# Key block of the retention branch moved behind a product of another item, gate stores on ScalarE's queue, value stores issued one group later

## The chip, the cores and the metric

The kernel runs on one core of a Trainium2 chip. The metric is the device time of one execution in microseconds (us); the median of several timed runs counts. The engines are named as the profile names them: PE (TensorE, matmuls), DVE (VectorE), ACT (ScalarE), POOL (GpSimd) and SP (SyncE, which only issues transfers here).

## The reference, cut to what matters

Two layers of a trunk over a sequence of 512 rows of 1024 float32 channels. Each layer begins with one wide projection of x, and the work around the change is this projection:

```python
for l in range(DEPTH):                                  # DEPTH = 2
    h = jnp.einsum('bsd,de->bse', x, w_in[l])
    rq, rk, rv, rg, cq, ck, cv, dq, dk, dv, gates = jnp.split(h, splits, axis=-1)
    o_a = _retention(rq, rk, rv, rg, ret_norm_g[l])     # rotary on rq and rk, 4 heads
    o_b = _chunk_attention(cq, ck, cv, ca_rel_bias[l])
    o_c = _diff_attention(dq, dk, dv, lam, lambda_init, da_norm_g[l])
    g = jax.nn.sigmoid(gates + b_merge[l]).reshape(B, S, N_BRANCHES, D)
    merged = sum(g[:, :, i] * (o_i @ w_i) for each of the three branches)
    x = _layer_norm(DEEPNORM_ALPHA * x + merged @ w_out[l], ...)
    x = _layer_norm(DEEPNORM_ALPHA * x + swiglu_ffn(x), ...)
```

## The kernel before, in words

**Numbers and weights.** Every float32 operand is carried as a pair of float32r tiles, a high half and a low half (names ending in h and l), and a float32 product is three matmuls (`mm3`, lines 122 to 124). Weights are streamed. A block of 1 MB (128 partitions by 2048 numbers) is loaded by a DMA from SP's queue into one of 4 staging tiles `st`, ACT copies its high half to `wh` and DVE subtracts to get the low half `wl` (line 271 and 272; 154 and 155 for blocks of 256 columns). The split pairs come from a pool of 3 (`AHEAD`), so a block can be split only when the third last has been used up by PE.

**Products from sums.** Four weight quarters and four quarters of x make one 2 by 2 product in seven block products rather than eight (Strassen-Winograd): `m1`, `m2`, `y`, `v`, `x`, `g`, `h`. The items of a projection pair carry a letter and one of these names: `w` projects the values CV and DV, `e` the gate of branch 0, `p` and `q` the retention's RV and RG. `m1`, `m2` and `h` use plain x on PE; `y` and `x` need the left sums of x (`s12`, function `s_left`), `v` and `g` the right sums (`s43`, `s_right`), which DVE and ACT make. Weight sums are made either by DVE in the staging tile (lines 233, 239 and 260) or by an accumulating DMA on POOL's queue (`more`, line 178). A letter with `a` or `c` (`w.a`, `w.c`, `e.c`, `p.a`) is such a load made ahead: `e.c`, for example, loads the block of `e.g` and accumulates a second quarter into it. PSUM results are copied by ACT (`tc`, line 761), combined by DVE (lines 766, 771 and 776) and passed on: values are split once more and stored to DRAM (`v_away`, line 882), gate halves go through a tanh and are stored (`gate_part`, line 1080; `gate_done`, line 1069, for other gates).

**Retention's queries and keys.** RQ and RK are blocks of 256 columns each. Their PSUM results go through a rotary (`rotary`, lines 400 to 404: ACT copies, DVE multiplies and adds) and a split (`rqkh`, `rqkl`). In both layers the item `u_first` makes both blocks of the first two heads. In layer 0 it is also the start of the program: `first_blocks` issues the loads of both weight blocks in quarters of 256 KB, with one tile of the transposed input xT between each two, and the splits of these in the same alternation (lines 613 and 614 for xT).

**What sets the order.** The kernel holds a list of items (`start` and the list behind it, from line 1143); `run_items` walks it in program order, fetches the weights of coming items ahead, and after each half of an item `between` runs a group of side work (sums, loads ahead, the second layer's layer-norm outputs in natural order, `natural`). A scheduler then reorders instructions within each engine's stream by its own priorities, keeping dependencies; every engine and every DMA queue runs its stream in order.

Of the kernel before, what the change touches and what calls it, by code (L numbers as in the profile page):

```python
# [17 lines left out]
P = 128  # L18
# [38 lines left out]
def trunk(ctx, tc, x_in, xT_in, w_in, ret_norm_g, da_norm_g, lq1, lk1, lq2, lk2, w_a, w_b, w_c, b_merge, w_out,  # L57
# [506 lines left out]
    pending = []  # L564

    def between():

        if pending:
            for fn in pending.pop(0):
                fn()  # L570
# [28 lines left out]
    def first_blocks(*specs):  # L599

        wts = [Wt(*sp, later=True) for sp in specs]
        for k in range(0, KT, 2):
            for i, wt in enumerate(wts):
                wt.load(k, k + 2)
                xfs[0][k + i] = g(name="xf")
                nc.sync.dma_start(xfs[0][k + i], xT_in[P * (k + i):P * (k + i) + P])
        for k in range(0, KT, 2):
            for i, wt in enumerate(wts):
                src, pr = xfs[0][k + i], Pair("xT")
                xTs[0][k + i] = pr  # L610
                for ins in wt.split(k, k + 2):
                    tc.keep_in_program_order(ins)
                tc.keep_in_program_order(nc.scalar.copy(pr.hi, src))
                tc.keep_in_program_order(nc.vector.tensor_sub(pr.lo, src, f(pr.hi)))  # L614
        return wts
# [9 lines left out]
    def layer(l):  # L625
# [82 lines left out]
        def u_first():  # L708

            def fn(*wts):  # L710
                banks = [[bank("pt") for _ in range(2)] for _ in range(2)]
                if l == 0:
                    ret_tables()
                    for k in range(KT):
                        for w, b in zip(wts, banks):
                            for j in range(2):
                                a, c = xT[k], slice(P * j, P * j + P)
                                mm3(b[j], w.hi[:, k, c], w.lo[:, k, c], a.hi, a.lo, k == 0, k == KT - 1)
                    quarters(0)
                    for k in range(4):  # L720
                        s_left(k)()
                    vectors()
                for i, w in enumerate(wts):
                    for j in range(2):
                        if l:
                            proj_T(xT, w, P * j, ps=banks[i][j])
                        rqk_done((rq, rk)[i], j, banks[i][j])
                        between()

            return [([wcols(c, 256)], KT) for c in (RQ, RK)], fn  # L730
# [140 lines left out]
        def v_away(dst, wd):  # L871


            def done(t, c):
                for hf in range(2):
# [6 lines left out]
                    nc.sync.dma_start(dst[t, hf], f(s))  # L882
# [180 lines left out]
        def gate_done(br, d, ps, away=True):  # L1063
# [3 lines left out]
            if away:  # L1067
                th[br, d] = dram.tile([P, 512], F32, name=f"th{l}_{br}_{d}")
                nc.sync.dma_start(th[br, d], t)

        def gate_part(br, d, hf, c):
# [3 lines left out]
            for i in range(2):  # L1075
# [4 lines left out]
                nc.sync.dma_start(th[br, d + i][:, 256 * hf:256 * hf + 256], s[:, o])  # L1080
# [62 lines left out]
        if l == 0:  # L1143
            start = [(u_first(), [], [], [w["a"]], [columns]), (w["m1"], [s_right(0)], [s_right(1)]),
                     (w["m2"], [s_right(2)], [s_right(3)]), (e["m1"],), (e["m2"], [w["c"]]), (w["y"], [lam]), (w["v"],)]
        else:
            turned, natural = ([functools.partial(fn, i) for i in range(4)] for fn in hooks[l])
            start = [(w["m1"], [ret_tables, vectors], turned[:2]), (w["m2"], turned[2:]),
                     (u_first(), [w["a"], s_left(0)], [s_left(1), s_left(2)], [s_left(3)], [columns]),
                     (e["m1"], [s_right(0)], [s_right(1)]), (e["m2"], [s_right(2), w["c"]], [s_right(3)]),  # L1150
                     (w["y"], [natural[0]], [natural[1]]), (w["v"], [natural[2], lam], [natural[3]])]
# [323 lines left out]
```

## Time and profile before

| | |
|---|---|
| timed runs, median (lowest to highest) | 1929.14 us (1928.84 to 1929.17), 3 runs |
| the profiled execution's own time | 1930.13 us |
| its span in the profile | 1928.0 us, granted clock 0.987 |
| PE busy | 1871.7 us, 97% |
| DVE, ACT, POOL busy | 1374.2, 991.9, 130.5 us |
| DMA | 306.07 MB, 159 GB/s in the mean |

How to read the rows of the profile that follow: a row of a timeline is start, duration, engine, line, operation, output and inputs, number of instructions, and in brackets the engine's idle time just before it with the instruction that ended that idle time. A row of windows gives for a stretch its length, then each engine's busy time and number of instructions, the granted TensorE clock as a share of full speed, the DMA engines' share and GB/s. A row of the groups gives busy time and mean nanoseconds of one instruction, then the idle time before them. Tile names are those of the program without their numbers: `pf` and `pt` are PSUM banks of block products and of projections, `psr` of the retention's scores.

### The profile page before, as it was taken

How to read it: one execution, taken by the hardware profiler on the slowest of the kernel's cores; microseconds unless marked ns; L12 is line 12 of the kernel's file. 1: busy time of each engine (PE TensorE's matmuls, PEld its weight loads, DVE VectorE, ACT ScalarE, POOL GpSimd, SP SyncE). 2: the span in 40 equal slices, each digit the busy share in tenths (PEclk: the TensorE clock that was granted, in tenths of full speed). 3: DMA queues.
4: the chain of work that ended last, by engine and by line, in shares of the span. 5: the costliest groups of instructions: out<-in, count | busy, mean ns of one | idle time of the engine just before them, and what ended most of it. 6: DMA issues, size and time to landing. Idle time of an engine off the chain costs nothing. (4 is left out here: it accounts for less than half of the span.)

```text
span 1928.0 us, 24006 instructions
## 1 busy us (share of the span) xinstructions
PE 1871.7 (97%) x9090; PEld 1573.8 (82%) x9090; DVE 1374.2 (71%) x2069; ACT 991.9 (51%) x1605; POOL 130.5 (7%) x153
## 2 busy tenths in 40 slices
PE   9879999999999999999997799999999999999998
PEld 7768888888888888888886688888888888888886
DVE  6747766767766777888688577666677667778886
ACT  5545555566743544654264454555676435455541
POOL 2000000000000000010020000000000000100100
PEclk9989999999999999999998899999999999999999
DMA  9787344332235676787377863443421456777871
GB/s 285 190 248 199 98 150 151 93 132 77 66 131 153 174 187 187 180 230 204 127 189 212 240 187 108 138 137 110 136 77 45 153 157 171 181 190 204 210 196 44
DMA packets 223283, 306.07 MB, mean 159 GB/s; under 512 B 8900, under 2 KB 111392, under 8 KB 223168
## 3 DMA queue, kind: packets, MB, share of 16 engines
q1 hardware_dynamic: 192832, 245.40, 38.3%
q0 software_dynamic: 30336, 59.15, 17.8%
q8 instruction: 71, 1.16, 0.2%
q14 instruction: 44, 0.36, 0.1%
HBM read 281.39 MB, written 23.12 MB: 158 GB/s over the span
## 5 line engine op out<-in xcount | busy, mean ns | idle before, releaser
L272 DVE TENSOR_TENSOR wl<-st,wh 128x2048 fp32r<-128x2048 f32 x140 | 320.2, 2290 | 147.6 <-ACT wh L271 147.0
L271 ACT CAST wh<-st 128x2048 fp32r<-128x2048 f32 x140 | 267.2, 1911 | 240.1 <-PE pf L124 101.9
L122 PE MATMUL pt<-xTh,wh 128*128 128x512 f32 x832 | 327.0, 394 | 1.1 <-ACT wh L154 0.9
L123 PE MATMUL pt<-xTl,wh 128*128 128x512 f32 x832 | 324.1, 389 | 1.9 <-DVE xTl L614 1.9
L124 PE MATMUL pt<-xTh,wl 128*128 128x512 f32 x832 | 324.3, 390 | 0.0
L155 DVE TENSOR_TENSOR wl<-st,wh 128x1024 fp32r<-128x1024 f32 (+1 forms) x188 | 200.1, 1084 | 60.6 <-ACT wh L154 54.6
L154 ACT CAST wh<-st 128x1024 fp32r<-128x1024 f32 (+1 forms) x188 | 172.3, 940 | 111.7 <-PE pt L123 34.3
L123 PEld LDWEIGHTS pt<-xTl,wh 128*128 128x128 f32 x832 | 156.4, 188 | 33.4 <-DVE xTl L614 2.2
L124 PEld LDWEIGHTS pt<-xTh,wl 128*128 128x128 f32 x832 | 156.2, 188 | 33.0
L122 PEld LDWEIGHTS pt<-xTh,wh 128*128 128x128 f32 x832 | 156.2, 188 | 33.0 <-ACT wh L154 1.4
L122 PE MATMUL pf<-wh,xTh 128*128 128x512 f32 x336 | 132.8, 395 | 1.5 <-ACT rph L106 0.8
L123 PE MATMUL pf<-wl,xTh 128*128 128x512 f32 x336 | 131.3, 391 | 0.5 <-DVE wl L272 0.3
L124 PE MATMUL pf<-wh,xTl 128*128 128x512 f32 x336 | 131.0, 390 | 0.0
L761 ACT COPY tc<-pf 128x512 f32<-128x512 f32 x96 | 54.9, 588 | 76.1 <-PE pf L124 69.7
L123 PE MATMUL pf<-wl,s12h 128*128 128x512 f32 x224 | 87.7, 391 | 3.2 <-DVE wl L272 3.2
L122 PE MATMUL pf<-wh,s12h 128*128 128x512 f32 x224 | 87.9, 395 | 1.6 <-ACT wh L271 1.6
L122 PE MATMUL pf<-wh,s43h 128*128 128x512 f32 x224 | 87.4, 390 | 0.0
L124 PE MATMUL pf<-wh,s12l 128*128 128x512 f32 x224 | 87.3, 390 | 0.0
L123 PE MATMUL pf<-wl,s43h 128*128 128x512 f32 x224 | 87.2, 389 | 0.0
L124 PE MATMUL pf<-wh,s43l 128*128 128x512 f32 x224 | 87.2, 389 | 0.0
L122 PEld LDWEIGHTS pf<-wh,xTh 128*128 128x128 f32 x336 | 63.1, 188 | 16.5 <-ACT rph L106 1.6
L123 PEld LDWEIGHTS pf<-wl,xTh 128*128 128x128 f32 x336 | 63.2, 188 | 13.5 <-DVE wl L272 1.5
(338 smaller groups left out, 4082.7 us busy)
## 6 DMA issues: line engine op xcount, KB each, us to landing
st<-in_w_in SPq DMA_DIRECT2D x62, 1024.0 KB, 5.2
st<-in_w_ffn_in SPq DMA_DIRECT2D x38, 1024.0 KB, 5.7
st<-in_w_in POOLq DMA_DIRECT2D x20, 1024.0 KB, 10.4
st<-in_w_ffn_in POOLq DMA_DIRECT2D x20, 1024.0 KB, 10.8
st<-in_w_ffn_out SPq DMA_DIRECT2D x20, 1024.0 KB, 7.5
st<-in_w_in SPq DMA_DIRECT2D x32, 512.0 KB, 5.0
st<-in_w_ffn_out POOLq DMA_DIRECT2D x16, 1024.0 KB, 9.0
st<-in_w_ffn_in SPq DMA_DIRECT2D x24, 512.0 KB, 6.4
```

The lines of the kernel that those rows point to most:

```text
L122: nc.tensor.matmul(ps, lh, rh, start=start, stop=False, skip_group_check=onto)
L123: nc.tensor.matmul(ps, lh, rl, start=False, stop=False, skip_group_check=onto)
L124: nc.tensor.matmul(ps, ll, rh, start=False, stop=stop, skip_group_check=onto)
L154: return [nc.scalar.copy(self.hi[:, a:b], self.st[:, a:b]), nc.vector.tensor_sub(self.lo[:, a:b], self.st[:, a:b], f(self.hi[:, a:b]))]
L155: nc.vector.tensor_sub(self.lo[:, a:b], self.st[:, a:b], f(self.hi[:, a:b]))]
L271: nc.scalar.copy(self.hi, st)
L272: nc.vector.tensor_sub(self.lo, st, f(self.hi))
L761: nc.scalar.copy(t[to, j], ps)
```

## The change

It has four parts. (1) `u_first` makes only the RQ block and is used only in layer 0; `first_blocks` therefore starts the program with one weight block and all eight xT tiles. (2) RK becomes an item of its own (`u_rqk(rk, RK, 0)`) and comes behind `w.y`, so that `w.m1`, `w.m2`, `e.m1` and `e.m2`, which need no sums of x, stand ahead of `w.y`. The items behind it change places: before `w.v, w.x, e.y, w.g, e.v, w.h, p.m1`, now RK, `w.v, e.y, w.x, e.v, w.g, p.m1, w.h`. In layer 1 RQ is an item of its own too, and the side work (`columns`, the sums, `natural`) is handed to later groups. (3) The value stores of `v_away` are put in a list and issued by `between` one group later, still on SP's queue. (4) The gate stores `th` are issued from ACT's queue (`nc.scalar.dma_start`) instead of SP's.

```diff
 def between():
+    for fn in stores.pop(0):
+        fn()
+    stores.append([])
     if pending:
...
-    def first_blocks(*specs):
-        wts = [Wt(*sp, later=True) for sp in specs]
+    def first_blocks(spec):
+        wt = Wt(*spec, later=True)
         for k in range(0, KT, 2):
-            for i, wt in enumerate(wts):
-                wt.load(k, k + 2)
-                xfs[0][k + i] = g(name="xf")
+            wt.load(k, k + 2)
+            for i in (k, k + 1):
+                xfs[0][i] = g(name="xf")
...
-            return [([wcols(c, 256)], KT) for c in (RQ, RK)], fn
+            return [([wcols(RQ, 256)], KT)], fn
...
-                    nc.sync.dma_start(dst[t, hf], f(s))
+                    stores[-1].append(functools.partial(nc.sync.dma_start, dst[t, hf], f(s)))
...
-                nc.sync.dma_start(th[br, d], t)
+                nc.scalar.dma_start(th[br, d], t)
...
-                nc.sync.dma_start(th[br, d + i][:, 256 * hf:256 * hf + 256], s[:, o])
+                nc.scalar.dma_start(th[br, d + i][:, 256 * hf:256 * hf + 256], s[:, o])
...
         if l == 0:
-            start = [(u_first(), [], [], [w["a"]], [columns]), (w["m1"], [s_right(0)], [s_right(1)]),
-                     (w["m2"], [s_right(2)], [s_right(3)]), (e["m1"],), (e["m2"], [w["c"]]), (w["y"], [lam]), (w["v"],)]
+            start = [(u_first(), [], [w["a"]]), (w["m1"], [], [s_right(0)]), (w["m2"], [columns], [s_right(1)]),
+                     (e["m1"], [], [s_right(2)]), (e["m2"], [s_right(3)], [w["c"]]), (w["y"], [lam])]
...
-                     (w["y"], [natural[0]], [natural[1]]), (w["v"], [natural[2], lam], [natural[3]])]
+                     (w["y"], [lam], [natural[0]])]
...
-            (w["x"],), (e["y"],), (w["g"], [p["a"]]), (e["v"], [e["c"]]), (w["h"],),
-            (p["m1"], [s_dh(0)]), (e["x"],), (p["y"], [], [s_r1(0)]), (e["g"],), (p["v"], [s_dh(1)], [p["c"]]), (e["h"],),
+            (u_rqk(rk, RK, 0), *([[natural[1]], [natural[2]]] if l else [])), (w["v"], *([[natural[3]]] if l else [])),
+            (e["y"],), (w["x"],), (e["v"], [p["a"]]), (w["g"], [e["c"]]), (p["m1"], [s_dh(0)]), (w["h"],), (e["x"],),
+            (p["y"], [], [s_r1(0)]), (e["g"],), (p["v"], [s_dh(1)], [p["c"]]), (e["h"],),
```

At the start of layer 0 the copy of the last xT tile's high half stands on ACT directly behind the split of w.m1's whole block, after the change as before.

**ACT in layer 0 around w.y.** Here is ACT's stream of before, from the third rotary of `u_first` (`sw`, `rqkh`) to the copies of e.m1 (`tc11_412` and `tc11_434` are w.m1's; `wh_571` is a split of the block in `st_569`):

```order
L400 COPY sw_355<-pt_189 64x512 x2
L271 CAST wh_571<-st_569 128x2048
L106 CAST rqkh_362<-rot_358 128x512
L400 COPY sw_369<-pt_190 64x512 x2
L106 CAST rqkh_376<-rot_372 128x512
L761 COPY tc11_412<-pf_399 128x512
L106 CAST s43h_417<-sb_414 128x512
L761 COPY tc11_434<-pf_421 128x512
L271 CAST wh_645<-st_569 128x2048
```

This is ACT's stream after the change, at the place where RK's work begins. `tc11_319` and `tc11_334` are w.m1's copies, `wh_561` is w.v's split, `wh_610` is e.y's, and `tc11_437` and `tc11_466` are the copies of e.m1:

```order
L760 COPY tc11_334<-pf_321 128x512
L106 CAST s43h_339<-sb_336 128x512
L271 CAST wh_561<-st_559 128x2048
L106 CAST vhl_363<-tc11_319 128x4x64
L106 CAST vhl_367<-tc11_319 128x4x64
L106 CAST vhl_391<-tc11_334 128x4x64
L106 CAST vhl_395<-tc11_334 128x4x64
L271 CAST wh_610<-st_299 128x2048
L106 CAST s43h_404<-sb_401 128x512
L760 COPY tc11_437<-pf_412 128x512
L760 COPY tc11_466<-pf_441 128x512
```

The third and fourth rotary are gone from this place, and the copies of e.m1 stand behind e.y's split. DVE's adds of e.m2 to these copies are what frees the PSUM banks that RK's matmuls use.

**POOL's accumulating transfers in layer 0.** These are six in a row of before: `st_392` in the first, third and fifth row is the block of chain e (the fifth makes e.h's), `st_609` is w.c's, `st_866` p.a's, and `st_924` in the last row is e.c's:

```order
L178 DMA st_392<-in_w_in 128x4x512
L178 DMA st_609<-in_w_in 128x4x512
L178 DMA st_392<-in_w_in 128x4x512
L178 DMA st_866<-in_w_in 128x4x512
L178 DMA st_392<-in_w_in 128x4x512
L178 DMA st_924<-in_w_in 128x4x512
```

The same stretch after the change, where `st_299` is the block of chain e, `st_556` w.c's, `st_864` p.a's and `st_918` e.c's:

```order
L178 DMA st_299<-in_w_in 128x4x512
L178 DMA st_556<-in_w_in 128x4x512
L178 DMA st_299<-in_w_in 128x4x512
L178 DMA st_864<-in_w_in 128x4x512
L178 DMA st_918<-in_w_in 128x4x512
L178 DMA st_299<-in_w_in 128x4x512
```

The last two have changed places: e.c's transfer no longer stands behind the one that makes e.h's block. In layer 1 the order of these two is as before.

**DVE in layer 1.** Here is DVE's stream of before around the add that frees a bank for e.y (`tc11_8525`, from e.m2); `z` are the passes of `natural`:

```order
L553 TENSOR_TENSOR z_7011<-z_7011,bc_7786 128x512
L404 TENSOR_TENSOR rot_8476<-rot_8476,sw_8473 128x512
L554 TENSOR_TENSOR z_7011<-z_7011,bc_7790 128x512
L553 TENSOR_TENSOR z_7012<-z_7012,bc_7787 128x512
L112 TENSOR_TENSOR rqkl_8481<-rot_8476,rqkh_8480 128x512
L304 TENSOR_TENSOR sb_8527<-xf_8090,sa_8351 128x256
L305 TENSOR_TENSOR sb_8527<-xf_8066 128x256
L766 TENSOR_TENSOR tc11_8525<-tc11_8525,pf_8575 128x512
L554 TENSOR_TENSOR z_7012<-z_7012,bc_7791 128x512
L553 TENSOR_TENSOR z_7013<-z_7013,bc_7786 128x512
```

And this is where the passes of `natural` begin after the change; `wl_8715` is the low half of w.x's split, `s43l_8569` the last of the right sums:

```order
L305 TENSOR_TENSOR sb_8565<-xf_8077 128x256
L686 TENSOR_TENSOR nlam_8601<-le_8599 128x1
L272 TENSOR_TENSOR wl_8715<-st_8572,wh_8714 128x2048
L112 TENSOR_TENSOR s43l_8569<-sb_8565,s43h_8568 128x512
L687 TENSOR_SCALAR nlam_8601<-nlam_8601 128x1
L553 TENSOR_TENSOR z_7004<-z_7004,bc_7779 128x512
L553 TENSOR_TENSOR z_7010<-z_7010,bc_7779 128x512
L554 TENSOR_TENSOR z_7004<-z_7004,bc_7783 128x512
L553 TENSOR_TENSOR z_7005<-z_7005,bc_7780 128x512
L402 TENSOR_TENSOR rot_8658<-pt_8630,cosr_8162 128x512
```

All passes of `natural` now come behind the adds of e.m2, the last sums and w.x's split, and RK's rotary stands among them.

More of the change, by code (lines that the diff above doesn't have):

```diff
@@ L564, in trunk @@
     pending = []
+    stores = [[], []]
     def between():
+        for fn in stores.pop(0):
+            fn()
+        stores.append([])
         if pending:
@@ L708, in u_first, with fn @@
         def u_first():
[L710 to L723, printed above, removed]
-                    for j in range(2):
[L725 to L728, printed above, removed]
-            return [([wcols(c, 256)], KT) for c in (RQ, RK)], fn
+            def fn(wt):
+                banks = [bank("pt") for _ in range(2)]
+                ret_tables()
+                for k in range(KT):
+                    for j in range(2):
+                        a, c = xT[k], slice(P * j, P * j + P)
+                        mm3(banks[j], wt.hi[:, k, c], wt.lo[:, k, c], a.hi, a.lo, k == 0, k == KT - 1)
+                quarters(0)
+                vectors()
+                for k in range(4):
+                    s_left(k)()
+                for j in range(2):
+                    rqk_done(rq, j, banks[j])
+                    between()
+            return [([wcols(RQ, 256)], KT)], fn
         def s_left(k):
```

18 lines of the change are left out of this document (9 added, 9 removed).

## The prediction

> **What bounds the kernel now.** I read the page first, then windows of the span, then the PE's waits, and last the timelines of the engines at the stretches that wait.
>
> ```profile
> span 1928.0 us, 24006 instructions
> PE 1871.7 (97%) x9090; PEld 1573.8 (82%) x9090; DVE 1374.2 (71%) x2069; ACT 991.9 (51%) x1605; POOL 130.5 (7%) x153
> ...
> core 0: us, PE busy (x) PEld busy (x) DVE busy (x) ACT busy (x) POOL busy (x), PEclk, DMA share, GB/s
> 0.00:240.00 240.00, 215.49 (x1115) 184.50 (x1116) 162.39 (x193) 124.13 (x177) 23.70 (x35) 0.96 0.73 204
> 240.00:960.00 720.00, 719.24 (x3430) 601.88 (x3429) 515.95 (x823) 372.92 (x623) 40.44 (x46) 1.00 0.53 150
> 960.00:1240.00 280.00, 258.48 (x1337) 220.63 (x1337) 199.88 (x258) 149.10 (x231) 24.68 (x29) 0.96 0.64 177
> 1240.00:1930.00 690.00, 678.50 (x3213) 566.76 (x3211) 495.96 (x796) 345.75 (x577) 41.65 (x45) 0.99 0.51 144
> ```
>
> The PE is the bound: it is busy for 1871.7 of 1928.0 us. The change leaves its matmuls as they are and can only alter the idle 56 us. The windows show where those lie: 24.5 us in the first 240 us (the start of layer 0) and 21.5 us between 960 and 1240 (the start of layer 1). The change works in exactly these two stretches. The granted clock is 0.96 there, so idle time costs twice: it is lost, and afterwards the PE runs slower.
>
> Smaller windows give each stall's price, as idle time plus busy time times the missing clock:
>
> ```profile
> 49.00:62.00 13.00, 8.50 (x49) 8.30 (x50) 12.16 (x18) 5.02 (x8) 1.27 (x1) 0.76 0.76 186
> 68.00:88.00 20.00, 17.00 (x97) 14.47 (x96) 12.73 (x16) 11.44 (x19) 1.27 (x1) 1.00 0.85 237
> 123.00:145.00 22.00, 10.84 (x59) 9.86 (x58) 13.61 (x13) 10.61 (x14) 1.28 (x1) 0.69 0.63 189
> 1010.00:1047.00 37.00, 26.96 (x126) 22.29 (x125) 32.29 (x48) 15.66 (x24) 1.27 (x1) 0.86 0.59 177
> 1081.00:1103.00 22.00, 11.66 (x60) 10.70 (x59) 13.39 (x13) 10.61 (x14) 1.28 (x1) 0.69 0.67 199
> ...
> 25.21 0.50 PE L123 MATMUL pt<-xTl,wh 128*128 128x512 f32 x1 [1.92 <-DVE xTl L614]
> 49.70 0.39 PE L122 MATMUL pf<-xTh,wh 128*128 128x256 f32 x1 [1.60 <-DVE rot L402]
> 49.93 0.28 PE L123 MATMUL pf<-xTl,wh 128*128 128x256 f32 x1
> 56.63 0.58 PE L122 MATMUL pf<-xTh,wh 128*128 128x256 f32 x1 [3.79 <-DVE rot L402]
> 57.01 0.41 PE L123 MATMUL pf<-xTl,wh 128*128 128x256 f32 x1
> ...
> 128.22 0.58 PE L122 MATMUL pf<-s43h,wh 128*128 128x256 f32 x1 [4.92 <-ACT wh L271]
> 136.27 0.48 PE L122 MATMUL psr<-rqkh 128*128 128x128 f32 x1 [4.71 <-DVE rtmp L817]
> 1029.23 0.55 PE L122 MATMUL pf<-s12h,wh 128*128 128x256 f32 x1 [3.53 <-DVE tc L766]
> 1033.21 0.58 PE L124 MATMUL pf<-s12h,wl 128*128 128x256 f32 x1 [3.22 <-DVE wl L272]
> ```
>
> Layer 0: e.m2 loses 13.0 − 8.5 = 4.5 us idle, 2.0 us at clock 0.76, and the 1.6 us before: 8.1. The stretch of w.x, e.y and w.v (68 to 88) loses 3.0. e.g (123 to 145) loses 11.2 idle and 0.31 × 10.84 = 3.4: 14.5. Layer 1: w.y to w.v (1010 to 1047) loses 10.0 + 3.8 = 13.8, e.g 10.3 + 3.6 = 13.9. These five places are 53 us. The gap of 3.79 us was followed by matmuls of 0.41 instead of 0.28 us; the one of 1.60 was not.
>
> **The change part by part.** *The start of layer 0.* One weight block less stands ahead of w.m1's block, but the last xT tile still waits behind it.
>
> ```profile
> 3.68 0.62 ACT L154 CAST wh<-st 128x512 fp32r<-128x512 f32 x1 [1.67 <-DMA st<-in_w_in]
> 20.32 1.91 ACT L271 CAST wh<-st 128x2048 fp32r<-128x2048 f32 x1 [4.08 <-DMA st<-in_w_in]
> 22.13 0.61 ACT L613 CAST xTh<-xf 128x512 fp32r<-128x512 f32 x1
> 22.26 2.29 DVE L272 TENSOR_TENSOR wl<-st,wh 128x2048 fp32r<-128x2048 f32 x1 [4.58 <-ACT wh L271]
> 24.47 0.69 DVE L614 TENSOR_TENSOR xTl<-xf,xTh 128x512 fp32r<-128x512 f32 x1
> ```
>
> From the first piece to w.m1's block, 19 pieces of 256 KB arrive in 16.6 us, 0.88 each. Four fewer put w.m1's block at about 16.8. ACT's split, DVE's split (2.29) and the low half of xT (0.69) then end near 21.7, and RQ's last six matmuls at 23.1. RQ alone needs 11.0 us from 5.0 on, so it waits 7 where both blocks waited 2.9; with about 2 us at low clock the start costs +6. In return only two rotaries, not four, stand in front of e.m2. Adding the rows' durations up, its two banks come 1.3 and 2.0 us late in place of 8.1: −4.8. Net +1.2.
>
> *RK behind w.y, layer 0.* RK's first matmul needs the bank that the add for e.m2 releases (tc11 on DVE). That add needs ACT's copy of e.m1, and the copy now stands behind e.y's split on ACT, which waits for one of three split buffers, so for the end of w.y.
>
> ```profile
> L272 DVE TENSOR_TENSOR wl<-st,wh 128x2048 fp32r<-128x2048 f32 x140 | 320.2, 2290 | 147.6 <-ACT wh L271 147.0
> L271 ACT CAST wh<-st 128x2048 fp32r<-128x2048 f32 x140 | 267.2, 1911 | 240.1 <-PE pf L124 101.9
> L761 ACT COPY tc<-pf 128x512 f32<-128x512 f32 x96 | 54.9, 588 | 76.1 <-PE pf L124 69.7 <-issue 3.2 <-PE ph L1265 2.0
> L766 DVE TENSOR_TENSOR tc<-tc,pf 128x512 f32<-128x512 f32 x32 | 21.8, 685 | 21.3 <-PE pf L124 20.4 <-ACT tc L761 0.9
> ```
>
> After w.y ends come the split (1.9), the high half of a right-hand sum (as long as a copy, 0.6), the copy (0.6) and the add (0.7): 3.8 as lower end, with DVE free. Two passes of 2.29 ahead of the add, a split and a block addition, make 8.4 as upper end. I take 7.4, near the upper end because DVE was busy for 12.16 of 13 us in the window at 49. With 2.7 at low clock (the 2.0 of that window, and a little more for the longer gap) this is +10.1. It is a new wait, and nothing hides it. Behind RK the banks and splits of w.x, e.y and w.v have been ready for 11 us of RK, so the 3.0 lost there goes: −3.0.
>
> *e.g, layer 0.* Its block is loaded by SP and then gets a second quarter added by an accumulating transfer on POOL's queue.
>
> ```profile
> 91.95 6.07 SPq L882 DMA_DIRECT2D v<-vhl  x6
> 107.89 2.58 POOL L178 DMA_DIRECT2D st<-in_w_in  x2 [17.59 <-DVE wl L272]
> 126.27 1.90 ACT L271 CAST wh<-st 128x2048 fp32r<-128x2048 f32 x1 [14.60 <-DMA st<-in_w_in]
> st<-in_w_in SPq DMA_DIRECT2D x62, 1024.0 KB, 5.2
> st<-in_w_in POOLq DMA_DIRECT2D x20, 1024.0 KB, 10.4
> ```
>
> Before, e.h's accumulation stood first and waited for e.x's split; e.c's was issued with it at 107.9 and landed 17 us later, against 10.4 in the median. Now e.c stands first. The work up to w.x ended at 88 before and is 8.3 later by the terms so far: 96.3. ACT and DVE then split p.m1 (4.2), which lets SP issue e.c's load near 101; it lands 5 to 6 us later, and the accumulation goes out while e.h's still waits. By the median and a few microseconds of overlap it lands near 120 to 122, ahead of p.y's end (123.3 before, since PE idled 4.92 up to 128.22; now 131.6). PE then finds wh and wl ready. I credit −12 of 14.5; if it lands only after 126 (17 us again), the stall keeps 10, because four gate activations and four gate stores on ACT now stand between e.g's split and p.v's, and rtmp follows p.v's split on DVE.
>
> *Layer 1, w.y to w.v.* DVE had 33 instructions in 20 us, among them the multiply-add passes of `natural`, between the adds and splits that PE waited for:
>
> ```profile
> 1020.00:1040.00 20.00, 12.61 (x61) 11.02 (x60) 19.96 (x33) 10.26 (x15) 1.27 (x1) 0.74 0.59 170
> ```
>
> These passes now stand behind w.x's split. By the durations above w.y and RK run without a wait; then w.x's wh waits for RK's end behind the activations (2.9 us idle), and its wl for 3.4 more; with 2.7 at low clock 9.0 in place of 13.8: −4.8. The Trainium skill, "TensorE: Matmul & The Clock Gate", section "What's actually happening", says that the clock is halved only after an idle window of about 3.4 us. The 3.79 and 1.60 us gaps agree with it. By it these two gaps, each below or at that length, would cost no clock, and the sum would be 2.7 us lower.
>
> *e.g, layer 1.* Here e.c's accumulation still stands behind e.h's.
>
> ```profile
> 1080.27 0.39 PE L122 MATMUL psr<-rqkh 128*128 128x512 f32 x1
> 1066.71 2.58 POOL L178 DMA_DIRECT2D st<-in_w_in  x2 [18.28 <-DVE wl L272]
> 1084.62 1.90 ACT L271 CAST wh<-st 128x2048 fp32r<-128x2048 f32 x1 [13.62 <-DMA st<-in_w_in]
> ```
>
> It was issued 13.6 us ahead of p.y's end (the psr matmul at 1080.27 follows it); I place it 15 to 18 ahead, since p.y comes earlier by less than e.x's split does. With the same 17 us it is still late by 0 to 3, and rtmp behind the gate stores keeps 5 and the clock 2.7. I take 9.5 in place of 13.9: −4.4, bounds 0 and −10.
>
> *The queues.* A DMA issue takes 0.4 to 1.0 us on SP (six in 6.07); ACT shows none, so I price a gate store at 0.4, with 1.0 as upper end, four ahead of each of three splits: included above. Four stores wait for earlier SP transfers; these were issued 10 us and more before by the same steps, so I take 0 (rival below). The Trainium skill, "DMA: Bandwidth & Descriptors", section "Issuing engines are not separate DMA queues", says that transfers from any engine share the same 16 DMA engines and a second issuer saves only issue time; no run here shows it yet. By it the move to ACT's queue earns no bandwidth, and I credited none.
>
> **Sum.** 1.2 + 10.1 − 3.0 − 12.0 − 4.8 − 4.4 = −12.9 us on the profiled 1930.13 us (span 1928.0 and 2.1 around it): 1917.2. The median of the three timed runs, 1929.14, lies 1.0 lower: 1916.
>
> **The rivals.** *Slower: e.g stays late while RK's wait comes on top.* If e.c's accumulation again takes 17 us in layer 0 (it shares the engines with e.h's and with loads), or p.v's split waits behind the gate stores on ACT for SP's value stores, e.g keeps its 14.5 and 13.9. The terms are then 1.2 + 10.1 − 3.0 − 4.8 = +3.5, and with a wait of 8.4 at RK and nothing won in layer 1's middle +9: 1933 to 1938. It decides from a landing after about 126 in layer 0. For it speaks that both traced pairs of accumulations took 17 us; against, that they were issued together. Chance 0.20.
>
> *No change.* e.g in layer 0 gains 4 to 8 rather than 12, and layer 1 nothing in e.g: 1.2 + 10.1 − 3.0 − 6 − 4.8 = −2.5, which is 1926.6; with half of the last gain gone, 1930: 1926 to 1931. Chance 0.15.
>
> *Larger gain.* The tc11 copy comes before the split's wait bites, or the bank is free as it is in my walk of layer 1, and RK costs nothing: −12.9 − 10.1 = −23: 1906, and 1901 with layer 1's e.g cleared. Chance 0.15.
>
> **How the numbers follow.** My forecast, 1909 to 1923, holds 0.50. The range 1902 to 1935 takes in the larger gain and most of the slower case. A difference under 0.2% (3.9 us) can't be told from no change here. Faster by more than that: 0.50 + 0.15 and 0.02 of the middle case, 0.67; within, 0.14; slower, 0.19.
>
> **What would show it.** Right: RQ's last matmuls wait about 5 to 7 us for xTl near 17 to 22 us; a gap of 4 to 8 us with tc as releaser stands between w.y and RK in layer 0 and none in layer 1; no wait for wh over 2 us at e.g in layer 0, PE idle under 21 us in the first 240 us; in layer 1 two gaps at w.x of about 3 us; PE busy total falls by the recovered clock. Wrong: ACT idle behind a gate store; e.g in layer 0 waiting over 4 us for wh; idle time anywhere between 240 and 960 us, which was 0.8.

## The result, and the profile after

| | median (lowest to highest), us | against the kernel before |
|---|---|---|
| before | 1929.14 (1926.30 to 1929.17), 5 runs | |
| changed kernel | 1936.55 (1934.83 to 1943.42), 5 runs | 1.0049, 95% interval 1.0029 to 1.0070 |

The change makes the kernel slower by 0.3 to 0.7%, where 1916 was forecast; the range ended at 1935. The profiled execution of the changed kernel took 1934.83 us, the shortest of its five, against 1930.13 before. First the page and four windows, as they were shown of before:

```profile
span 1933.0 us, 23955 instructions
PE 1872.8 (97%) x9090; PEld 1573.7 (81%) x9090; DVE 1373.2 (71%) x2067; ACT 992.6 (51%) x1603; POOL 130.4 (7%) x153
...
0.00:240.00 240.00, 218.29 (x1130) 186.52 (x1131) 165.10 (x194) 127.27 (x176) 23.83 (x35) 0.96 0.74 208
240.00:960.00 720.00, 719.24 (x3430) 602.16 (x3429) 515.29 (x826) 373.29 (x624) 40.47 (x45) 1.00 0.53 149
960.00:1240.00 280.00, 252.07 (x1291) 213.84 (x1290) 195.69 (x252) 143.26 (x221) 24.47 (x28) 0.94 0.65 176
1240.00:1935.00 695.00, 683.24 (x3245) 571.14 (x3243) 497.16 (x797) 348.82 (x583) 41.63 (x45) 0.99 0.51 143
```

PE's busy time is the same (1871.7 before). In the first 240 us idle time fell, from 24.5 to 21.7 us. Between 960 and 1240 it rose, from 21.5 to 27.9, and the clock there fell from 0.96 to 0.94. Between 240 and 960 nothing changed. So layer 0 won a little and layer 1 lost more. The end of e.h, the item behind the five places of the prediction, marks the two parts:

| end of e.h on PE, us | layer 0 | layer 1 | from one to the other |
|---|---|---|---|
| before | 155.7 | 1114.0 | 958.2 |
| changed | 152.4 | 1118.4 | 966.0 |

Layer 0 gains 3.4 us in this execution, layer 1 gives back 7.8. PE's waits of the changed kernel (total, times, longest):

```profile
PE psr L122 <- DVE rtmp L816: 10.3, 2, 5.2
PE pf L122 <- ACT wh L271: 7.7, 3, 5.2
PE pf L123 <- DVE wl L272: 6.2, 4, 2.7
PE pt L122 <- DVE tc L765: 6.1, 1, 6.1
PE pf L122 <- ACT s12h L106: 5.5, 1, 5.5
```

The same waits in PE's timeline of the changed kernel (the first four rows are layer 0):

```profile
20.55 0.79 PE L122 MATMUL pt<-xTh,wh 128*128 128x512 f32 x1 [3.91 <-ACT xTh L617]
51.75 0.50 PE L122 MATMUL pf<-wh,s12h 128*128 128x512 f32 x1 [0.83 <-DVE tc L765]
63.60 0.77 PE L122 MATMUL pt<-xTh,wh 128*128 128x512 f32 x1 [6.11 <-DVE tc L765]
134.43 0.48 PE L122 MATMUL psr<-rqkh 128*128 128x128 f32 x1 [5.16 <-DVE rtmp L816]
...
998.49 0.66 PE L123 MATMUL pf<-wl,s12h 128*128 128x512 f32 x1 [1.20 <-DVE wl L272]
1005.41 0.80 PE L122 MATMUL pf<-wh,s12h 128*128 128x512 f32 x1 [5.53 <-ACT s12h L106]
1025.08 0.73 PE L122 MATMUL pf<-wh,s12h 128*128 128x512 f32 x2 [2.09 <-ACT wh L271]
1028.48 0.80 PE L123 MATMUL pf<-wl,s12h 128*128 128x512 f32 x1 [2.67 <-DVE wl L272]
...
1077.93 0.50 PE L123 MATMUL pf<-wl,s12h 128*128 128x512 f32 x1 [1.82 <-DVE wl L272]
1089.88 0.58 PE L122 MATMUL pf<-s43h,wh 128*128 128x256 f32 x1 [5.24 <-ACT wh L271]
1092.21 0.58 PE L124 MATMUL pf<-s43h,wl 128*128 128x256 f32 x1 [1.53 <-DVE wl L272]
1098.38 0.47 PE L122 MATMUL psr<-rqkh 128*128 128x128 f32 x1 [5.17 <-DVE rtmp L816]
```

In layer 0 the wait for weights at e.g is gone, as forecast; the wait of the scores' bank (`psr`, freed by the decay multiplication `rtmp`) stays. In layer 1 w.y, forecast to run without a wait, waits three times, 0.53 (row not shown), 1.20 and 5.53 us; p.y waits too, 0.41 (not shown) and 1.82, and e.g as before. What these wait for is seen on ACT and POOL in layer 1:

```profile
994.21 1.90 ACT L271 CAST wh<-st 128x2048 fp32r<-128x2048 f32 x1 [10.13 <-DMA st<-in_w_in]
1087.93 1.90 ACT L271 CAST wh<-st 128x2048 fp32r<-128x2048 f32 x1 [8.12 <-DMA st<-in_w_in]
...
974.78 2.71 POOL L178 DMA_DIRECT2D st<-in_w_in  x2
1059.09 1.27 POOL L178 DMA_DIRECT2D st<-in_w_in  x1 [36.07 <-DMA st<-in_w_in]
1063.14 1.27 POOL L178 DMA_DIRECT2D st<-in_w_in  x1 [2.78 <-DMA st<-in_w_in]
1064.76 1.28 POOL L178 DMA_DIRECT2D st<-in_w_in  x1 [0.35 <-issue]
```

The split at 994.21 is w.y's. Its block is w.a, the second of the two accumulations issued from 974.78 on; it landed some 18 us later, and ACT stood idle for 10.1 us. The low half on DVE and the sums `s12`, which stand behind this split on ACT, came late with it. Before, RK's 11 us lay in front of w.y and covered this landing: w.y's split waited there for the end of RK on PE, which frees its buffer, and not for a transfer. These are its row and POOL's row of p.a's accumulation before:

```profile
998.21 1.91 ACT L271 CAST wh<-st 128x2048 fp32r<-128x2048 f32 x1 [1.29 <-PE pt L123]
...
1047.16 1.28 POOL L178 DMA_DIRECT2D st<-in_w_in  x1 [12.20 <-ACT vhl L106]
```

The change took the cover away. p.a's accumulation, which p.y needs, now goes out at 1059.09, 12 us later than before. The split at 1087.93 is e.g's: e.c's accumulation went out at 1064.76, the third within 6 us, and took 23 us.

### The profile page after: what moved, and what is told of

Read it like the earlier page. It is cut to its first block, busy times and chain, and to the rows that moved or that the text cites. A ratio compares the mean times of both kernels' runs of the same rounds, so it can differ in the third digit from the quotient of the medians.

```text
span 1933.0 us, 23955 instructions
## 1 busy us (share of the span) xinstructions
PE 1872.8 (97%) x9090; PEld 1573.7 (81%) x9090; DVE 1373.2 (71%) x2067; ACT 992.6 (51%) x1603; POOL 130.4 (7%) x153
## 5 line engine op out<-in xcount | busy, mean ns | idle before, releaser
L122 PE MATMUL pt<-xTh,wh 128*128 128x512 f32 x832 | 329.1, 396 | 10.1 <-DVE tc L765 6.1
L124 PEld LDWEIGHTS pf<-wh,xTl 128*128 128x128 f32 x336 | 63.1, 188 | 13.6 <-DVE xTl L112 0.5
## 6 DMA issues: line engine op xcount, KB each, us to landing
st<-in_w_in POOLq DMA_DIRECT2D x20, 1024.0 KB, 11.6
```

The costliest lines, as they stand in the source:

```text
L122: nc.tensor.matmul(ps, lh, rh, start=start, stop=False, skip_group_check=onto)
L124: nc.tensor.matmul(ps, ll, rh, start=False, stop=stop, skip_group_check=onto)
```

## The experiments

Two theories at the start. **A**: layer 1 loses because w.a's accumulation lands late and because p.a's, e.h's and e.c's run beside one another before e.g. **B**: the gate stores on ACT's queue hold up ACT, and that is the loss. Below, "the step" is the time from e.h's end in layer 0 to its end in layer 1; it was 958.2 us before and is 966.0 in the changed kernel. Each ratio is against runs of the kernel before on the same chip (medians 1929.2 to 1930.3 us).

**e1: gate stores back on SP.** The changed kernel with both lines undone:

```diff
-                nc.scalar.dma_start(th[br, d], t)
+                nc.sync.dma_start(th[br, d], t)
```

> The changed kernel with both gate stores back on SP's queue; nothing else undone. Theory A (layer 1 loses its time because w.y's split waits for w.a's accumulating transfer, 10.1 us of idle ACT, and because three accumulations overlap before e.g): the gate stores matter little, 1935 to 1937 us, and the psr waits in e.g (5.2 us in both layers) shorten by 1 to 2 at most. Theory B (the gate stores on ACT's queue, which wait there for value stores ahead of p.v's split, are the loss): 1929 to 1932 us, the psr waits fall to 2 us or less.

Measured: 1942.02 us (1934.68 to 1943.95), 1.0049 [1.0031, 1.0067]. The median lies above both expectations. The step is 965.3, as in the changed kernel, and the `psr` waits stay at 6.4 and 4.7, so theory B falls for the gate stores. The Trainium skill, "DMA: Bandwidth & Descriptors", section "Issuing engines are not separate DMA queues", says that a second issuing engine adds no bandwidth; nothing here speaks against it. Something new shows: the profiled run took 1943.95, and RK in layer 0 waited 11.6 us instead of 6.1; e.h in layer 0 ended 9.4 us later than in the changed kernel's trace, about as much as the time is longer.

**e2 and e3: one layer in the old order.** e2 keeps the new order in layer 0 alone, e3 in layer 1 alone; stores as changed in both:

```diff
+        if l in (0,):       # e2; (1,) in e3
             start, mid = items in the changed order
+        else:
+            start, mid = items in the order of before
```

> The new order and start in layer 0 alone; layer 1 has the order of before (RQ and RK together, w.v before w.x, natural at w.y and w.v). Stores are as in the changed kernel in both layers. Theory A: layer 0 gains 3.4 us and layer 1 loses nothing: 1925 to 1927 us. Theory B: the stores, which stay moved, cost most of what the changed kernel lost: 1932 to 1936 us.

> The counterpart: the order of before in layer 0, the new one in layer 1, stores as in the changed kernel. Theory A: layer 1's loss of 7.9 us stands alone: 1936 to 1940 us, not faster than the changed kernel. Theory B: about 1932 to 1936 us, and the two halves lose alike.

Measured: e2 1934.24 us (1928.22 to 1937.32), 1.0016 [1.0004, 1.0027]; e3 1937.55 (1934.41 to 1940.72), 1.0032 [1.0021, 1.0044]. e3 falls in theory A's range. e2 falls in theory B's, but its trace shows RK's wait in layer 0, 11.3 us, and not a cost of the stores. The old order in layer 1 brings the step back to 959.7. With the new one alone it is 970.1, with much the same waits at w.y. The larger part of the loss belongs to layer 1's order; layer 0's, alone, brings no gain, and the two ratios add up to the changed kernel's (0.16% and 0.32%, together 0.48%, against 0.49%). No run takes back the later value stores alone. The traces speak against them as the loss: with the old order and moved stores e.h ended in layer 0 at 153.4 in e3, against 155.7 before, and the step in e2 is 1.5 us above that of before.

**e4: w.a's accumulation with w.m1 in layer 1.**

```diff
-            start = [(w["m1"], [ret_tables, vectors], turned[:2]), (w["m2"], turned[2:]),
-                     (u_rqk(rq, RQ, 0), [w["a"], s_left(0)], [s_left(1), s_left(2)]),
+            start = [(w["m1"], [ret_tables, vectors, w["a"]], turned[:2]), (w["m2"], turned[2:]),
+                     (u_rqk(rq, RQ, 0), [s_left(0)], [s_left(1), s_left(2)]),
```

> The changed kernel, but in layer 1 the load and accumulation of w.a are asked for with w.m1 rather than with RQ. Theory A: w.a's accumulation lands before RQ ends, ACT's idle 10.1 us before w.y's split and the PE waits of 0.5, 1.2 and 5.5 us at w.y go, with about 3 us of low clock: 1925 to 1929 us. Theory B: w.y's wait goes, but another takes its place: 1934 to 1937 us.

Measured: 1934.34 us (1928.43 to 1938.11), 1.0018 [1.0008, 1.0029]; the step falls to 959.9, by 6.1. The median lies in theory B's range, since RK in layer 0 waited 12.1 us in this trace; the ratio fell by 0.31%, 6 us, as the step did. Of w.y's waits one is left, now because a sum on ACT stands behind a split that waits 3.64 us for another transfer:

```profile
1012.24 0.50 PE L122 MATMUL pf<-wh,s12h 128*128 128x512 f32 x1 [2.79 <-ACT s12h L106]
```

The first half of theory A holds.

**e5: w.c's accumulation behind RK in layer 0.** RK's wait had been 6.1 us in one trace and 11 to 12 in three. In these three (e1, e2, e4) the split of w.v's block waited 6.6 to 7.4 us for its transfer, in the changed kernel's trace 1.4. ACT's rows of the changed kernel and of e1:

```profile
53.13 1.91 ACT L271 CAST wh<-st 128x2048 fp32r<-128x2048 f32 x1 [1.38 <-DMA st<-in_w_in]
```

```profile
59.77 1.90 ACT L271 CAST wh<-st 128x2048 fp32r<-128x2048 f32 x1 [6.93 <-DMA st<-in_w_in]
```

That load is issued by SP at 47 to 48 us, up to 1.4 us behind w.c's accumulation on POOL (46.84 in the changed kernel). It took 5.8 us in the changed kernel's trace, 11.0 to 11.9 in those three and in e11, and 8.7 in e6, where RK waited 9.0. The edit moves the accumulation away:

```diff
-                     (e["m1"], [], [s_right(2)]), (e["m2"], [s_right(3)], [w["c"]]), (w["y"], [lam])]
+                     (e["m1"], [], [s_right(2)]), (e["m2"], [s_right(3)]), (w["y"], [lam])]
...
-            (u_rqk(rk, RK, 0), *([[natural[1]], [natural[2]]] if l else [])),
+            (u_rqk(rk, RK, 0), *([[natural[1]], [natural[2]]] if l else [[w["c"]]])),
```

> The changed kernel, but in layer 0 the load ahead of w.c is asked for with RK instead of after e.m2, so that its accumulating transfer doesn't start beside w.v's load. In four profiles taken since, RK waited 11.3 to 12.1 us for the add on DVE where the first profile showed 6.1, because w.v's load, issued within a microsecond of w.c's accumulation, took 12 us. Theory A2 (that meeting is what makes the runs differ by 8 us): RK's wait is 4 to 6.5 us, and the runs lie close together near 1934 to 1936 us. Rival (something else holds w.v's load): the wait stays at 11 to 12 us in some runs and the times spread over 8 us as before.

Measured: 1940.61 us (1939.07 to 1942.41), 1.0056 [1.0044, 1.0068]. The runs lie closer together (a spread of 3.3 us in place of 8.6) and the split of w.v waits for no transfer, but RK still waits 7.8 us and the level is not the lower one. DVE's rows of e5 give a reason: e.y's split now stands ahead of the add that frees RK's bank, where the changed kernel has it behind (add at 62.77, split at 65.24).

```profile
61.92 2.29 DVE L272 TENSOR_TENSOR wl<-st,wh 128x2048 fp32r<-128x2048 f32 x1
65.39 1.28 DVE L765 TENSOR_TENSOR tc<-tc,pf 128x512 f32<-128x512 f32 x2
```

The late load makes the long waits; it isn't the whole of RK's wait. The forecast missed.

**e6, e7 and e8: e.h's accumulation behind e.c's.** In the row of accumulations e.h's now stands behind e.c's. e6 does this in the changed kernel, e7 together with the edits of e4 and e5, e8 in the kernel before:

```diff
 class Chain:
     def x(self):
-        return self.take(1, 0)
+        return self.block(self.a)
+    def ahead_c(self):
+        self.c = self.load(0, 1)
+        tc.keep_in_program_order(self.more(self.c, 1, 1))
+    def ahead_h(self):
+        tc.keep_in_program_order(self.more(self.a, 1, 0))
...
-            (p["y"], [], [s_r1(0)]), (e["g"],),
+            (p["y"], [e["late"]], [s_r1(0)]), (e["g"],),
```

The class serves the feed-forward products too. In these three kernels those leave out six accumulations of 1 MB (50 of 56 are left; the expectation of e9 says four); e9 has them all.

> The changed kernel, but the accumulation that makes e.h's block is asked for with p.y and kept behind e.c's on POOL's queue in both layers. Theory A (e.g waits in layer 1 because e.c's transfer stands behind and beside others): e.c lands 8 to 12 us earlier in layer 1, the waits of 5.2, 1.5 and 5.2 us at e.g shrink to under 5 us together, 8 to 12 us less than the changed kernel by the same state of layer 0: 1926 to 1932 us. Rival (e.c is late because its load is issued late, by the staging tiles): at most 3 us less.

> The three repairs together on the changed kernel: w.a asked for with w.m1 in layer 1, w.c with RK in layer 0, e.h's accumulation behind e.c's. Theory A: the gains add, 6 to 7 us for w.a, 8 for w.c in the runs that had it and 8 to 12 for e.g: 1916 to 1922 us, faster than both kernels. Rival: the repairs free transfers that meet elsewhere: 1925 to 1930 us.

> The kernel before with only e.h's accumulation put behind e.c's. Theory A: e.g loses 14.5 and 13.9 us in the two layers for want of e.c's block; with that transfer first, half or more of it goes: 1912 to 1920 us. Rival (e.c's load is too late by itself): 1925 to 1929 us.

Measured: e6 1933.33 us (1929.98 to 1939.75), 1.0024 [1.0012, 1.0035], step 963.1; e7 1927.96 (1924.35 to 1930.92), 0.9985 [0.9976, 0.9993], step 955.8; e8 1923.50 (1923.28 to 1924.64), 0.9968 [0.9956, 0.9980], step 955.6. In e6 layer 1's wait for `wh` at e.g is gone, as the second half of theory A has it. But the step falls by 2.9 us and not by 8 to 12, and the time just misses the range: the `psr` wait of 5.0 us stays, and p.y waits 3.2 us where it waited 2.2 in the changed kernel. e7 lands in its rival's range, e8 between its two. And e8, the old order with the one repair, is better than e7, the new order with three. What stays at e.g in e8 is above all one wait in each layer:

```profile
133.63 0.48 PE L122 MATMUL psr<-rqkh 128*128 128x128 f32 x1 [6.46 <-DVE rtmp L824]
1089.00 0.47 PE L122 MATMUL psr<-rqkh 128*128 128x128 f32 x1 [6.59 <-DVE rtmp L824]
```

**e9 and e10: the kernel before with the repair for the gates alone, and with the scores later too.** e9 puts e8's edit into a class of its own, `LateChain`, used by `u_gate_two` alone. e10 adds:

```diff
-            (p["y"], [e["late"]], [s_r1(0)]), (e["g"],), (p["v"], [s_dh(1)], [p["c"]]), (e["h"],),
+            (p["y"], [e["late"]]), (e["g"],), (p["v"], [s_dh(1)], [p["c"], s_r1(0)]), (e["h"],),
```

> The kernel before, with the last accumulation of the gate weights' sum (the block of e.h) taken out of e.x and queued on POOL behind the one of e.c, with e.c's held ahead of it; the feed-forward products keep all of theirs (unlike in the kernel before with this edit that ran earlier). Theory (in the kernel before e.g waits for weights because three accumulating transfers run beside one another): 1923 to 1925, about 6 below before, and e.g waits for no weights (wh, wl) in either layer; the waits for a score bank (rtmp, 6.46 and 6.59 us in the earlier run) stay. Rival (the earlier gain came from the four accumulations that the feed-forward products left out): 1929 to 1931, the time of before.

> The same, and the decay scores s_r1(0) go from behind the second half of p.y to behind the second half of p.v, two products later. Theory (what is left at e.g is the wait of the scores' bank for the DVE multiplication L816, with the slow clock behind it, and it is set by the scores' place): the waits of 6.5 and 6.6 us go, and the time falls by 6 to 12 us more, to 1912 to 1918. Rival (the bank chain only moves along: the scores wait the same where they stand now): within 1.5 us of the run with the late accumulation alone, and waits of 5 to 7 us on rtmp in p.v or e.h.

Measured: e9 1923.04 us (1920.33 to 1924.71), 0.9961 [0.9949, 0.9973]; e10 **1912.86 us** (1909.83 to 1913.15), 0.9907 [0.9894, 0.9920]. e9 agrees with e8, so the gain isn't that of the left-out accumulations. Both fall in the range of their theory, and e10 beats both kernels. Windows around e.g, first e9, then e10:

```profile
120.00:150.00 30.00, 22.43 (x123) 20.45 (x122) 20.16 (x18) 16.69 (x22) 1.28 (x1) 0.77 0.79 210
1070.00:1100.00 30.00, 23.41 (x134) 21.02 (x133) 16.50 (x16) 14.29 (x19) 1.28 (x1) 0.89 0.96 247
```

```profile
120.00:150.00 30.00, 25.31 (x150) 23.29 (x149) 20.23 (x16) 15.77 (x19) 1.28 (x1) 0.89 0.85 218
1070.00:1100.00 30.00, 26.90 (x166) 23.85 (x165) 21.48 (x18) 16.96 (x23) 1.28 (x1) 1.00 0.95 260
```

PE's busy time rises by 2.9 and 3.5 us, and the clock from 0.77 to 0.89 and from 0.89 to 1.00. Idle time falls by 6.4 us, and busy time times the missing clock by 5.0 (5.2 and 2.6 in e9, 2.8 and 0 in e10). Together that is near the 10.2 us that the scores' move brings, and more than a third of it is clock. In layer 0 e.g still waits 4.7 us, now for sums (e.x's, on DVE) behind a split.

**e11: the changed kernel with w.a early, e.h late and the scores later.**

> The changed kernel with three repairs: w.a's accumulation issued with w.m1 in layer 1, e.h's accumulation behind e.c's, the scores s_r1(0) behind p.v. Theory (these were the three steps that my sum had wrong): no wait over 1.5 us for weights at w.y in layer 1 and at e.g in both layers, no rtmp wait in e.g; 1936.6 - 2.2 (w.a) - 3.2 (e.h) - 6 to 12 (scores) = 1919 to 1925, the order of the change then as good as that of before with the same repairs or up to 5 us worse by RK's wait in layer 0. Rival (the change itself is worth nothing and its waits move along): 1928 to 1934.

Measured: 1923.98 us (1918.03 to 1929.12), 0.9966 [0.9954, 0.9978]. The repairs bring 12.6 us, and the time falls in the expected range. The same repairs in the old order (which needs no earlier w.a) end 11.1 us lower. In e11's trace RK waits 11.7 us in layer 0.

**e12 and e13: RK behind w.v in layer 0.** In e12 the items are swapped:

```diff
-            (u_rqk(rk, RK, 0), ...), (w["v"], ...),
+            *([(u_rqk(rk, RK, 0), ...), (w["v"], ...)] if l else [(w["v"],), (u_rqk(rk, RK, 0),)]),
```

> The changed kernel with RK behind w.v instead of w.y in layer 0; layer 1 as changed. RK's waits for a pt bank (6 to 12 us) end with the sums L765 of e.m2, which stand on DVE behind w.v's split; w.v itself takes pf banks. Theory (a lack of pt banks while the eviction queue is behind): RK's wait goes to under 2 us, and w.v waits only for its own split, 0 to 3 us: layer 0 gains 4 to 8 us and the time is 1929 to 1933. Rival (ACT and DVE are simply behind by that much, and whatever stands there waits): w.v waits 5 to 11 us for its split or its bank, and the time is 1935 to 1938.

Measured: 1947.97 us (1945.04 to 1951.36), 1.0093 [1.0078, 1.0107], outside both expectations. The run didn't test them: the scheduler set 40 of RK's 48 matmuls ahead of w.v's again. (The expectation was loose on one point: all PSUM tiles come from one pool of eight banks; w.v takes no new ones because it adds onto w.y's.) e13 holds the written order by `tc.keep_in_program_order` on the matmuls of both items.

> The changed kernel with RK behind w.v in layer 0, its matmuls and w.v's kept in the order in which they are written (in the run before, 40 of RK's 48 matmuls still stood ahead of w.v's). Theory (the eight banks are full at RK: w.m1, e.m1, w.y and e.m2 hold two each, and RK needs two that only e.m2's sums on DVE give back, while w.v adds onto w.y's two and needs none): RK waits under 2 us, w.v 0 to 3 us for its split, layer 0 gains 4 to 8 us against the changed kernel, 1929 to 1933. Rival (DVE and ACT are late whoever comes next): w.v waits 5 to 8 us for its split and the time is 1935 to 1938.

Measured: 1947.06 us (1946.38 to 1947.79), 1.0089 [1.0075, 1.0103]. PE's and ACT's rows of e13 (L764 is the copy of a bank by ACT, L158 the split of RK's block in halves):

```profile
73.32 0.79 PE L124 MATMUL pf<-wh,s43h 128*128 128x512 f32 x1 [11.59 <-ACT tc L764]
...
58.75 1.05 ACT L158 CAST wh<-st 128x1024 fp32r<-128x1024 f32 x1 [3.16 <-DMA st<-in_w_in]
72.68 1.07 ACT L764 COPY tc<-pf 128x512 f32<-128x512 f32 x2 [1.06 <-issue]
```

RK doesn't wait any more, but w.v does, for 11.6 us: it adds onto w.y's banks, and ACT must have copied these first. w.y ended at 61.7; its copies came at 72.7, behind splits, activations and gate stores, and ACT had itself lost 3.16 us to the landing of RK's block. So it isn't a lack of banks that is special to RK. At this place ACT and DVE are some 10 us behind PE, and whatever comes next meets them. The bank theory falls; the rival holds in kind, though its time was 9 us too low.

**e14 and e15: the repaired forms.** e14 is e13 with the repairs of e11; e15 has layer 0 in the old order and layer 1 in the new, with the same repairs.

> The same together with the three repairs (w.a's accumulation with w.m1 in layer 1, e.h's accumulation behind e.c's, the scores behind p.v). With the theory 1924.0 - 4 to 8 = 1916 to 1920, and a narrower spread, since RK's wait, which differs from run to run, is gone; by the rival 1922 to 1926.

> Layer 0 in the order of before, layer 1 in the changed order, with the three repairs. Theory (the changed order in layer 1 is worth nothing once its weights come in time: in the traces PE is busy 263.1 us from 960 to 1240 with the changed order repaired and 264.8 with the order of before repaired): 1913 to 1917, the old order with the repairs (1912.9) plus 0 to 4. Rival (my term of -4.8 at w.y to w.v in layer 1 was right and was only covered by w.a's late weights): 1906 to 1910.

Measured: e14 1929.39 us (1927.08 to 1931.19), 0.9999 [0.9990, 1.0008], w.v waiting 12.1 us: above both expectations and worse than e11, as e13 lets one expect. e15 1918.42 (1917.08 to 1920.53), 0.9940 [0.9926, 0.9953], 5.6 us above e10, a little outside both expectations on the slow side. The step is 953.3 in e15 and 947.5 in e10. The end of e.x, the item ahead of p.y, tells where layer 1 loses this. Counted from e.h's end in layer 0, e.x ends after 916.6 us in e15 and 919.4 in e10, so up to there the new order is 2.8 us ahead. Other traces agree: 916.0 to 917.2 in the five with the new order and w.a early (e4, e7, e11, e14, e15), 919.2 to 920.9 in the five with the old order (before, e2, e8, e9, e10). Then p.y ends 11.3 us behind e.x in e15 and 5.5 in e10. What is left in e15 at w.y and w.x, then at p.y, and POOL's row for the block that p.y waits for:

```profile
1003.99 0.50 PE L122 MATMUL pf<-wh,s12h 128*128 128x512 f32 x1 [2.57 <-ACT s12h L106]
1018.67 1.03 PE L122 MATMUL pf<-wh,s12h 128*128 128x512 f32 x2 [1.85 <-ACT wh L282]
1022.07 0.80 PE L123 MATMUL pf<-wl,s12h 128*128 128x512 f32 x1 [2.37 <-DVE wl L283]
...
1070.27 0.50 PE L122 MATMUL pf<-wh,s12h 128*128 128x512 f32 x1 [1.80 <-ACT wh L282]
1072.60 0.50 PE L123 MATMUL pf<-wl,s12h 128*128 128x512 f32 x1 [1.82 <-DVE wl L283]
...
1052.41 1.27 POOL L178 DMA_DIRECT2D st<-in_w_in  x1 [35.80 <-DMA st<-in_w_in]
```

That block is p.a. Its accumulation goes out 16 us ahead of e.x's end, where before and in e10 it is 28, and those of e.h and e.c follow within 7 us. In layer 1 of every trace with the new order p.y ends 7.9 to 11.9 us behind e.x, with the old order 5.5. So the new order of layer 1 wins about 3 us once w.a comes in time, and loses more at p.y. That p.a is the reason there is read from the traces; no run issued it earlier. (e15 keeps the moved stores, too, which e10 doesn't have.)

## Why the prediction was wrong

In layer 0 the mechanisms were the right ones and the largest term, e.g, was mis-sized. In layer 1 one step failed, one place was not in the sum at all, and both terms had the wrong sign. The parts, in the two profiled executions, by the ends of the items on PE:

| | forecast, us | measured, us |
|---|---|---|
| layer 0: start | +1.2 | +1.0 |
| layer 0: RK behind w.y | +10.1 | +7.8 |
| layer 0: from there to p.y's end | −3.0 | −4.6 |
| layer 0: e.g to e.h | −12.0 | −7.5 |
| layer 1: to e.x's end | −4.8 | +3.6 |
| layer 1: p.y | not in the sum | +2.8 |
| layer 1: e.g to e.h | −4.4 | +1.4 |
| sum | −12.9 | +4.5 |

The two executions differ by 4.7 us.

*Start of layer 0, +1.2: right.* RQ's last matmuls waited 3.91 and 1.6 us for xT, and w.y ended at 57.5. Before, it began at 61.9 after RK's 11.0 us; without these it would have ended near 56.5, so the start cost 1.0.

*RK behind w.y, +10.1: near for the trace that was taken, too low for other executions.* The wait came with its releaser as forecast, 6.11 us, and RK took 12.7 us instead of 11.0: 7.8 in all. In the traces of e1, e2, e4, e6 and e11, which have the same order in this stretch, the wait was 9.0 to 12.1. Two of the changed kernel's five runs, at 1940.1 and 1943.4 us, may be such cases; they have no trace. The step took the order on ACT and DVE as the whole cause. It left out the transfer for w.v's split, ahead in that order, and its collision with w.c's accumulation.

*w.x, e.y and w.v, −3.0: right, and a little low.* PE has no wait there, and the stretch to p.y's end is 4.6 us shorter.

*e.g in layer 0, −12.0: mis-sized, about −7.5.* From p.y's end to e.h's end PE took 26.1 us in place of 33.6. e.c landed in time and PE had no wait for `wh`. What stayed is 5.16 us of `rtmp` and the slow clock behind it. The text had the reason, "rtmp follows p.v's split on DVE", and used it only for the case in which e.c is late; it holds in either. DVE's rows of the changed kernel:

```profile
131.49 2.29 DVE L272 TENSOR_TENSOR wl<-st,wh 128x2048 fp32r<-128x2048 f32 x1 [4.83 <-ACT wh L271]
133.69 0.68 DVE L816 TENSOR_TENSOR rtmp<-psr,dh 128x512 f32<-128x512 f32 x1
```

The multiplication that frees the bank stands behind a split for which DVE waited 4.8 us. Moving the scores in e10 took 10.2 us from both layers together, on top of what the weights' repair in e9 had brought. The prediction had booked nearly all of e.g's loss to the weights.

*Layer 1, w.y to w.v, −4.8: the step that failed is "w.y and RK run without a wait".* I had looked at the sums and splits in front of w.y and not at the landing of w.a, which RK's 11 us had covered. PE waited 0.53, 1.20 and 5.53 us there. The price by e4 is 6.1 us. The waits at w.x came as forecast (2.09 and 2.67 against 2.9 and 3.4). Without w.a's wait the term has the forecast's sign and about half its size: e.x ends 2.7 us earlier in e4 and in e15 than before.

*p.y in layer 1: not in the sum.* p.a's accumulation went out later, as shown above, and p.y waited 0.41 and 1.82 us: +2.8 in all. The prediction looked at e.c's transfer alone.

*e.g in layer 1, −4.4: wrong sign, about +1.4.* From p.y's end to e.h's end PE took 35.0 us in place of 33.5. I placed e.c's issue 15 to 18 us ahead of p.y's end. It was 18.7 ahead (1064.76 against 1083.44), but with three accumulations in flight the landing took 23 us, not 17.

*The queues, 0: right within what can be told.* Issuing a gate store took ACT 0.4 to 0.7 us. One of the prediction's signs of being wrong did show: at e.g in layer 0 ACT stood idle among the gate stores for value stores, 0.54 and 1.10 us. But e1, with the gate stores on SP, gained nothing.

The slower rival gave 1933 to 1938 and the median fell there. Its mechanism was half of it: e.g stayed late in layer 1 and kept `rtmp` in layer 0, and nothing was won in the middle of layer 1. But e.c landed in time in layer 0, at 120.8, where this rival needed a landing after 126; that the number fits is in part luck.

*The clock.* By the rule that the prediction cites from the Trainium skill, "TensorE: Matmul & The Clock Gate", section "What's actually happening", two gaps below about 3.4 us would cost no clock. At w.x in layer 1 the trace differs. The windows of the changed kernel show a granted clock of 1.00 up to 1025.9 and of 0.50 from 1026.0 to 1032.8. So it fell right at the start of the gap of 2.67 us, after the gap of 2.09 and 0.7 us of work. The matmuls behind were slow for 4.4 us, the first at 0.80 and eight at 0.63 us, until 0.40 was reached again:

```profile
1029.08 0.63 PE L124 MATMUL pf<-wh,s12l 128*128 128x512 f32 x1
...
1032.88 0.40 PE L123 MATMUL pf<-wl,s43h 128*128 128x512 f32 x1
```

At w.y the clock was 0.50 from 998.7 on, after gaps of 0.53 and 1.20 us alone and ahead of the one of 5.53. A gap of 2.04 us in layer 0, and one of 2.16 before (70.50), cost no clock: their windows show 1.00. Here the length of a single gap did not decide it; what did, the runs don't show.

*What stays open.* Why ACT and DVE fall 10 us behind at w.y in layer 0, and whether another order of DVE's sums and splits there would let RK go earlier, was not tried. Nor was p.a's accumulation in layer 1 issued earlier in any run. What decides whether w.v's load takes 6 or 12 us is not known either; the one short case began 0.35 us behind w.c's accumulation, the others 0.8 to 1.4 us.

## What to carry to other kernels

Before a product is taken out of one place, list the transfers that land under it; a product of 11 us moved away uncovers a landing of 18. Where a wait falls away, ask which release stands next on the same engine, and take credit for the gain only up to there. An accumulating transfer should go out when it is wanted next, not when its tile is free: e.h's in front of e.c's cost about 7 us, and one group of scores two products too early 10.

## What the runs showed of the hardware

Accumulating transfers of 1 MB of the projection's weights land after 10.4 us in the median of before. Of two issued within a microsecond, the second took 17 to 19 us at the projection (17.5 and 17.1 before, 18.6 in the changed kernel), but 13.4 to 13.9 in the feed-forward part, which the prediction's "both traced pairs" leaves out. Of three within 6 us the last took 23. A plain load of 1 MB issued up to 1.4 us behind an accumulating one took 5.8, 8.7 or 11.0 to 11.9 us in six kernels that have the same order there. With the accumulation moved behind RK it took 5.1 and 5.2 (e5 and e7), and the runs of e5 spread over 3.3 us, where those of the changed kernel spread over 8.6.
